# Four pairs of rows of a token group in seven products instead of three, with weight sums made partly by accumulating transfers

## The chip, the cores and the metric

The kernel runs on one core of a Trainium2 chip. The metric is the device time of one execution in microseconds. Work is done by TensorE (PE, with its weight loads PEld), VectorE (DVE), ScalarE (ACT) and GpSimd (POOL); SyncE (SP) issues most transfers, which 16 DMA engines carry out.

## What is computed

The reference is a decoder trunk of two layers for 256 tokens of width 2048. Layer 0 has a retention mixer, layer 1 a short gated convolution; each is followed by a SwiGLU feed-forward network (FFN) with 5632 hidden columns. Every sub-layer has an RMSNorm with a shift and a scale from a conditioning vector, and its output is gated and added to x.

```python
for i in range(DEPTH):
    mod = (c_act @ w_mod[i] + b_mod[i])[:, None, :]
    sh1, sc1, g1, sh2, sc2, g2 = jnp.split(mod, 6, axis=-1)
    h = (rms_norm(x, norm1_g[i]) * (1.0 + sc1) + sh1)
    y = retention_mixer(...) if i % 4 == 0 else short_conv_mixer(...)
    x = x + g1 * y
    h = (rms_norm(x, norm2_g[i]) * (1.0 + sc2) + sh2)
    x = x + g2 * swiglu(h, ffn_w_in[i], ffn_w_out[i])

def swiglu(h, w_in, w_out):
    a, b = jnp.split(h @ w_in, 2, axis=-1)
    return (jax.nn.silu(a) * b) @ w_out
```

The change touches the FFN of layer 1 only. Weights and data are float32.

## The kernel before, in words

**Weights.** All weights lie in `w_all` in the order of use, in chunks of 128 x 2048 (1 MB). `fetch` (L381) has SP load a chunk into one of three `raw` buffers (RAW_BUFS). `prepare` (L387) cuts a chunk into pieces: ACT casts a piece into its high part `hi` (L413), DVE subtracts to get the low part `lo` (L416). `hi` and `lo` have four buffers each (PART_BUFS). A product is three matmuls: data high by weights high, data high by weights low, data low by weights high. `take` (L430) hands pieces to the products and prepares up to two pieces ahead.

**Order.** PE's program is in the order in which the code is written. The instructions of the other engines are put in order by the scheduler when the program is built, and each engine works through its own list; SP issues its transfers in order too.

**The FFN of layer 1** has two parts, over 20 and 24 of the 44 tiles of hidden columns (PART_TILES). The first four tiles of part 0 are done in narrow products together with the norm. Then come groups of the first projection ("token groups"): four in part 0 and six in part 1, each over 512 columns of a and the 512 columns of b that belong to them. A group takes eight pairs of 128-row blocks of the weights (the rows are h's 2048 features), one chunk per pair. Each part ends with its output projections: two groups in part 0, one in part 1 followed by eight narrow products.

**Plain and in sevens.** A pair of row blocks (a, b) by two column blocks (c, d) for two tiles of tokens is eight products of 128 x 128 by 512, `triple` (L1187 to L1189): 24 matmuls. For some pairs (IN_SEVENS in the first projection, OUT_SEVENS in the output) the kernel uses a Strassen-Winograd form with seven products, 21 matmuls, whose inputs are sums of the four data blocks and sums of the four weight blocks. The data sums come from `seven_sums` (L629), once per pair of rows. The weight sums are made anew for each seven by DVE, in `prepare`, into the tile `sums`: L419, L423 and L425. Its four pieces have 512, 1024, 1024 and 1024 columns.

**Banks.** Eight PSUM banks stand in two lanes of four, which groups use in turn. A group's four result banks `x_banks` are in its own lane; the four banks m1, m5, m6, m7 of the sevens (shared by all sevens of a group) are in the other lane, which the group before has to leave.

**Behind a group.** After a group's last seven, ACT and DVE combine the m banks into `y` (L1237 to L1241). `middle` (L1269) then returns three steps that are called when so many tiles of the next group are done: the first half of the results (L1248: the group's banks are added; SiLU L1272, product L1273) after 8, the second half after 8 more, and `turned` after 16 more: PE transposes the results (L1259), ACT and DVE split them into `mids` (L1280, L1281), and where the output uses sevens ACT copies them to `full` (L1284) for `seven_sums`. A plain pair counts 16 tiles, a seven 14.

Of the kernel before, what the change touches and what calls it, by code (L numbers as in the profile page):

```python
# [10 lines left out]
F32 = mybir.dt.float32  # L11
# [3 lines left out]
ALU = mybir.AluOpType  # L15
PSUM = bass.MemoryType.PSUM

P = 128
# [7 lines left out]
DV = 512  # L26
# [38 lines left out]
class Group:  # L65
# [202 lines left out]
def trunk(ctx: ExitStack, tc: tile.TileContext, x_in, c_in, pos_in, w_mod, cols_in, tab_in, w_all, out):  # L268
# [96 lines left out]


    order = [(g, *b) for _, _, g in in_use_order() for b in g.taken()]
    pieces, at_col = [], 0
    for _, _, g in in_use_order():
        width = sum(w for _, _, w in g.blocks())  # L370
        for o in range(-at_col % HALF, width, HALF):
            i = (at_col + o) % CHUNK
            if not g.seven:
                pieces.append(("plain", i))
            elif i == 0:
                pieces += [("seven", n) for n in range(4)]
        at_col += width
    order.reverse()
    ready, used, raws, fetched, n_fetched = [], [0], [], [], [0]

    def fetch():  # L381
        raw = wpool.tile([P, CHUNK], F32, tag="raw", name=name("raw"), bufs=RAW_BUFS)
        nc.sync.dma_start(raw, w_all[n_fetched[0]])
        n_fetched[0] += 1
        fetched.append(raw)

    def prepare(between=None):  # L387
        if prepared[0] == len(pieces):
            return
        kind, i = pieces[prepared[0]]  # L390
        prepared[0] += 1
        if i == 0:
            if not fetched:
                fetch()
            raws[:] = [fetched.pop(0)]
            while first <= units[0] < early and len(fetched) < RAW_BUFS - 1 and n_fetched[0] < w_all.shape[0]:
                fetch()
        full = raws[0]
        if kind == "plain":
            raw = full[:, i : i + HALF]  # L400
        else:
            if i == 0:
                blocks[:] = [spool[0].tile([P, 4, DV], F32, tag="sums", name=name("sums"), bufs=1)]
# [9 lines left out]
        nc.scalar.copy(hi[:, :n], raw)  # L413
        if between:
            between()
        nc.vector.tensor_tensor(lo[:, :n], raw, hi[:, :n].bitcast(F32), op=ALU.subtract)  # L416
        ready.append((hi, lo, n))
        if kind == "seven" and i == 0:
            nc.vector.tensor_tensor(  # L419
                blocks[0][:, 0:2, :].rearrange("p a b -> p (a b)"), full[:, DV : 3 * DV], full[:, : 2 * DV],  # L420
                op=ALU.subtract,
            )
            nc.vector.tensor_tensor(t2, block[2], t1, op=ALU.subtract)  # L423
        elif kind == "seven" and i == 1:
            nc.vector.tensor_tensor(t4, block[3], t2, op=ALU.subtract)  # L425

    blocks, spool = [], []
    prepared = [0]

    def take(group, k, col, width=P):  # L430
# [200 lines left out]
    def seven_sums(full, tag):  # L631

        (a11, a21), (a12, a22) = [[full[:, i, t * P : (t + 1) * P] for t in range(2)] for i in range(2)]
        s = spool[0].tile([P, 4, P], F32, tag="ssum", name=name("ssum"), bufs=1)
        s1, s2, s3, s4 = [s[:, i, :] for i in range(4)]
        nc.vector.tensor_tensor(s1, a21, a22, op=ALU.add)
        nc.vector.tensor_tensor(s2, s1, a11, op=ALU.subtract)
        nc.vector.tensor_tensor(s3, a11, a21, op=ALU.subtract)
        nc.vector.tensor_tensor(s4, a12, s2, op=ALU.subtract)
        dst = spool[0].tile([P, 2, 4, P], F32R, tag=tag, name=name(tag), bufs=1)  # L640
        nc.scalar.copy(dst[:, 0], s)
        nc.vector.tensor_tensor(dst[:, 1], s, dst[:, 0].bitcast(F32), op=ALU.subtract)
        return dst
# [550 lines left out]
    def token_products(steps, act, sums_of, then):  # L1194
# [8 lines left out]
        for n, g in enumerate(steps):  # L1203
            first, last = n == 0, n == len(steps) - 1
            if not g.seven:
# [28 lines left out]
            if g is sevens[-1]:  # L1234
                m1, m5, m6, m7 = [flat(m_banks[i]) for i in ("m1", "m5", "m6", "m7")]
                y11, y12, y21, y22 = values = [value(f"y{i}") for i in range(4)]
                nc.scalar.copy(y11, m1)  # L1237
                nc.vector.tensor_tensor(y12, m6, y11, op=ALU.add)
                nc.vector.tensor_tensor(y21, m7, y12, op=ALU.add)
                nc.vector.tensor_tensor(y12, m5, y12, op=ALU.add)  # L1240
                nc.vector.tensor_tensor(y22, m5, y21, op=ALU.add)  # L1241
# [22 lines left out]
    def middle(values, finals, tag, at, mid, sums_of):  # L1264

        a1, b1, a2, b2 = values

        def product_of(t):
            finals[2 * t]()  # L1269
            finals[2 * t + 1]()  # L1270
            a, b = values[2 * t], values[2 * t + 1]
            nc.scalar.activation(a, a, AF.Silu)  # L1272
            nc.vector.tensor_tensor(b, b, a, op=ALU.mult)  # L1273

        def turned():
            pts = [turned_banks((b1, b2), tag, 2 * i) for i in range(2)]
            for i, pt in enumerate(pts):
                n = at + 2 * i
                t = mid[n // 2]
                nc.scalar.copy(t[:, :, 0, :], pt)  # L1280
                nc.vector.tensor_tensor(t[:, :, 1, :], pt, t[:, :, 0, :].bitcast(F32), op=ALU.subtract)  # L1281
                if n in sums_of:
                    full = fpool.tile([P, 2, S], F32, tag="full", name=name("full"), bufs=1)
                    nc.scalar.copy(full, pt)  # L1284
# [142 lines left out]
```

## Time and profile before

| | |
|---|---|
| runs of the kernel | median 2607.35 us of 3 (2607.01 to 2611.01) |
| the profiled execution, device time | 2605.66 us |
| its span, first to last instruction | 2603.9 us |
| mean granted TensorE clock | 0.998 |
| transfers | 687 MB, mean 264 GB/s |
| matmuls | 14341 |

In the page's forty slices PE shows a nine in all but the first and the last, and DVE goes from sevens and eights to nines in the second half; the DMA engines fall from six to eight tenths to five and six in the last third, which is the FFN of layer 1 (from 1878 us).

How to read it: a row of a group of instructions has line, engine, operation, output and input, shape and count, then busy time, the mean length of one in ns, and the idle time of the engine just before them with what ended it. Lengths of matmuls overlap, so their price is taken from the distance of their starts. In a timeline a row is start, length, engine, line, operation, tiles, shape and how many were merged; in square brackets stands the idle time before it and what ended it. A row of waits has who waited, for whom, total us, times and the longest.

### The profile page before, as it was taken

What the parts mean: (1) busy time and instruction counts of PE and PEld (TensorE: products, weight loads), DVE (VectorE), ACT (ScalarE), POOL (GpSimd) and SP (SyncE); (2) the same over time, 40 slices, a digit from 0 to 9 for tenths busy, and PEclk for the clock granted to TensorE, in tenths of its full rate; (3) what the DMA queues carried; (4) which work ended last, traced back from release to release, by engine and by line L of the source; (5) the groups of instructions that cost most, each with busy time, mean ns of one, the idle gap of its engine ahead of it and who ended that gap; (6) DMA issues with size and microseconds to landing.
All of it is one profiled execution on the core that took longest, in us unless ns stands there. A gap on an engine that the chain in (4) does not pass through costs nothing.

```text
span 2603.9 us, 36702 instructions
## 1 busy us (share of the span) xinstructions
PE 2571.1 (99%) x14341; PEld 2239.5 (86%) x14341; DVE 2178.4 (84%) x2751; ACT 1300.3 (50%) x1757; POOL 129.6 (5%) x230
## 2 busy tenths in 40 slices
PE   7999999999999999999999999999999999999998
PEld 5998889888889888888888898888898888888887
DVE  7998878787698887777777889888889999999984
ACT  5544543444456444334444454444565554555553
POOL 0000000120000010010000100000000000000000
PEclk9999999999999999999999999999999999999999
DMA  9976668777676887888887868877755555555553
GB/s 399 402 278 239 231 229 323 273 284 279 252 286 243 330 324 292 290 307 304 293 296 285 306 236 317 316 296 279 287 179 209 180 208 201 189 202 198 196 195 129
DMA packets 96945, 687.48 MB, mean 264 GB/s; under 512 B 10753, under 2 KB 12545, under 8 KB 13825
## 3 DMA queue, kind: packets, MB, share of 16 engines
q1 hardware_dynamic: 96194, 684.48, 71.2%
q8 instruction: 112, 1.84, 0.3%
q10 hardware_dynamic: 576, 0.66, 0.1%
q14 instruction: 63, 0.52, 0.1%
HBM read 682.99 MB, written 2.10 MB: 263 GB/s over the span
## 4 chain that ended last, share of the span: by engine, by line
PE 66%; issue 28%; DVE 3%; DMA 2%; ACT 1%; POOL 0%; SPq 0%; POOLq 0%; ACTq 0%; DVEq 0%
PE bank L475 29%; PE bank L478 15%; PE bank L514 4%; PE bank L513 4%; PE bank L515 4%; DMA raw<-w_all 2%; PE bank L499 1%; PE bank L498 1%; PE bank L500 1%; PE bank L688 1%; DVE lo L416 1%; PE bank L689 1%; PE bank L543 1%; PE bank L690 1%; PE bank L542 1%
## 5 line engine op out<-in xcount | busy, mean ns | idle before, releaser
L413 ACT CAST hi<-raw 128x1024 fp32r<-128x1024 f32 (+1 forms) x912 | 932.3, 1031 | 904.2 <-DMA raw<-w_all 268.3
L416 DVE TENSOR_TENSOR lo<-raw,hi 128x1024 fp32r<-128x1024 f32 (+1 forms) x912 | 1081.0, 1196 | 281.2 <-ACT hi L413 278.8
L475 PE MATMUL bank<-h,hi 128*128 128x512 f32 x2016 | 699.8, 391 | 0.0
L478 PE MATMUL bank<-h,lo 128*128 128x256 f32 x2016 | 564.4, 280 | 0.0
L475 PEld LDWEIGHTS bank<-h,hi 128*128 128x128 f32 x2016 | 377.0, 187 | 82.5
L327 DVE SCALAR_TENSOR_TENSOR raw<-raw,cb 128x2048 f32<-128x2048 f32 x160 | 365.8, 2286 | 33.0 <-DMA raw<-w_mod 32.6
L478 PEld LDWEIGHTS bank<-h,lo 128*128 128x128 f32 x2016 | 381.0, 189 | 0.0
L475 PE MATMUL bank<-mid,hi 128*128 128x512 f32 x922 | 321.1, 395 | 0.0
L478 PE MATMUL bank<-mid,lo 128*128 128x256 f32 x922 | 256.1, 278 | 0.3 <-DVE lo L416 0.3
L475 PEld LDWEIGHTS bank<-mid,hi 128*128 128x128 f32 x922 | 172.9, 188 | 40.5
L513 PE MATMUL bank<-hi,h 128*128 128x512 f32 x512 | 201.7, 394 | 0.0
L514 PE MATMUL bank<-lo,h 128*128 128x512 f32 x512 | 200.9, 392 | 0.1
L515 PE MATMUL bank<-hi,h 128*128 128x512 f32 x512 | 200.0, 391 | 0.0
L1187 PE MATMUL bank<-hi,h 128*128 128x512 f32 x490 | 191.5, 391 | 0.0
L1189 PE MATMUL bank<-hi,h 128*128 128x512 f32 x490 | 190.7, 389 | 0.0
L1188 PE MATMUL bank<-lo,h 128*128 128x512 f32 x490 | 190.7, 389 | 0.0
L478 PEld LDWEIGHTS bank<-mid,lo 128*128 128x128 f32 x922 | 173.3, 188 | 0.6 <-DVE lo L416 0.6
L475 PE MATMUL bank<-rm,hi 128*128 128x512 f32 x496 | 173.0, 395 | 0.0
L413 ACT CAST hi<-sums 128x1024 fp32r<-128x1024 f32 x84 | 88.4, 1052 | 143.2 <-PE bank L1189 104.0
L416 DVE TENSOR_TENSOR lo<-sums,hi 128x1024 fp32r<-128x1024 f32 x84 | 102.8, 1223 | 50.4 <-ACT hi L413 50.1
L478 PE MATMUL bank<-rm,lo 128*128 128x256 f32 x496 | 137.7, 278 | 0.0
L515 PEld LDWEIGHTS bank<-hi,h 128*128 128x128 f32 x512 | 96.6, 189 | 20.7
(230 smaller groups left out, 4098.1 us busy)
## 6 DMA issues: line engine op xcount, KB each, us to landing
raw<-w_all SPq DMA_DIRECT2D x456, 1024.0 KB, 4.9
raw<-w_mod SPq DMA_DIRECT2D x192, 1024.0 KB, 5.5
x<-x_in SPq DMA_DIRECT2D x4, 512.0 KB, 5.2
decay<-tab_in SPq DMA_DIRECT2D x8, 128.0 KB, 3.4
out<-x SPq DMA_DIRECT2D x4, 256.0 KB, 3.2
out<-x ACTq DMA_DIRECT2D x3, 128.0 KB, 2.6
out<-x SPq DMA_DIRECT2D x1, 384.0 KB, 2.6
out<-x ACTq DMA_DIRECT2D x1, 256.0 KB, 3.2
```

The costliest lines, as they stand in the source:

```text
L327: nc.vector.scalar_tensor_tensor(raw, raw, 1.0, cb, op0=ALU.mult, op1=ALU.mult, accum_out=total)
L413: nc.scalar.copy(hi[:, :n], raw)
L416: nc.vector.tensor_tensor(lo[:, :n], raw, hi[:, :n].bitcast(F32), op=ALU.subtract)
L475: nc.tensor.matmul(pt, hi, h, start=fresh and k == g.ks[0], stop=False, skip_group_check=True)
L478: nc.tensor.matmul(pt[:, 1, :], lo, h[:, 0, :], start=False, stop=last and k == g.ks[-1], skip_group_check=True)
L498: nc.tensor.matmul(pt, hi, h[:, 0, :], start=first, stop=False, skip_group_check=True)
L513: nc.tensor.matmul(flat(pt), a[:, 0, :], hi, start=first, stop=False)
L514: nc.tensor.matmul(flat(pt), a[:, 0, :], lo, start=False, stop=False)
L515: nc.tensor.matmul(flat(pt), a[:, 1, :], hi, start=False, stop=last)
L1187: nc.tensor.matmul(flat(pt), a[:, 0, :], hi, start=first, stop=False, skip_group_check=True)
L1188: nc.tensor.matmul(flat(pt), a[:, 0, :], lo, start=False, stop=False, skip_group_check=True)
L1189: nc.tensor.matmul(flat(pt), a[:, 1, :], hi, start=False, stop=last, skip_group_check=True)
```

## The change

- IN_SEVENS of layer 1 goes from pairs 2, 4, 6 to pairs 2, 3, 5, 6. The output's sevens stay as they are.
- The form of the seven products changes signs, so that all weight sums are additions: B11 + B12, B22 + B12 and so on. The seven's blocks lie in another order in `w_all`, and the seven products come in another order.
- `fetch` issues three more transfers for a chunk that a seven uses: SP loads the first block again into a tile `sums` (128 x 512, two buffers instead of one of 128 x 4 x 512), POOL adds the third block onto the fourth inside `raw`, and POOL adds the fourth block onto `sums`. DVE makes the other two sums by two additions in place in `raw` (L424, L425 of the changed kernel). The pieces have 1024, 1024, 512 and 1024 columns; the last one reads what L424 and L425 have written.
- The first half of a group's results is worked on at once and no longer after 8 tiles, so the turning comes 24 tiles into the next group and not 32.

```diff
-IN_SEVENS = {0: (), 1: (2, 4, 6)}
+IN_SEVENS = {0: (), 1: (2, 3, 5, 6)}
+SUM_BUFS = 2
...
-            return [(a, c, DV), (a, d, DV), (b, d, DV), (b, c, DV)]
+            return [(a, c, DV), (b, c, DV), (b, d, DV), (a, d, DV)]
...
-        nc.sync.dma_start(raw, w_all[n_fetched[0]])
+        src = w_all[n_fetched[0]]
+        nc.sync.dma_start(raw, src)
+        if n_fetched[0] in seven_chunks:
+            sums = spool[0].tile([P, DV], F32, tag="sums", name=name("sums"), bufs=SUM_BUFS)
+            nc.sync.dma_start(sums, src[:, :DV])
+            nc.gpsimd.dma_start(raw[:, 3 * DV :], src[:, 2 * DV : 3 * DV], accum_op=ALU.add)
+            nc.gpsimd.dma_start(sums, src[:, 3 * DV :], accum_op=ALU.add)
+            summed_raw.append(sums)
...
-            block = [full[:, n * DV : (n + 1) * DV] for n in range(4)]
-            t1, t3, t2, t4 = [blocks[0][:, n, :] for n in range(4)]
-            if i < 2:
-                raw = full[:, 2 * DV * i : 2 * DV * i + (DV, 2 * DV)[i]]
-            else:
-                raw = blocks[0][:, 2 * i - 4 : 2 * i - 2, :].rearrange("p a b -> p (a b)")
+                sums_now[:] = [summed_raw.pop(0)]
+            raw = (full[:, : 2 * DV], full[:, 2 * DV :], sums_now[0], full[:, DV : 3 * DV])[i]
...
-        if kind == "seven" and i == 0:
-            nc.vector.tensor_tensor(
-                blocks[0][:, 0:2, :].rearrange("p a b -> p (a b)"), full[:, DV : 3 * DV], full[:, : 2 * DV],
-                op=ALU.subtract,
-            )
-            nc.vector.tensor_tensor(t2, block[2], t1, op=ALU.subtract)
-        elif kind == "seven" and i == 1:
-            nc.vector.tensor_tensor(t4, block[3], t2, op=ALU.subtract)
+        if kind == "seven" and i == 1:
+            b21, b22 = full[:, DV : 2 * DV], full[:, 2 * DV : 3 * DV]
+            nc.vector.tensor_tensor(b22, b22, sums_now[0], op=ALU.add)
+            nc.vector.tensor_tensor(b21, b21, b22, op=ALU.add)
...
-                ("m1", a11), (x_banks[1][0], s4), (x_banks[0][0], a12), ("m5", s1), ("m7", s3), ("m6", s2),
-                (x_banks[0][1], a22),
+                ("m1", a11), (x_banks[0][0], a12), (x_banks[1][0], s4), ("m7", s3), ("m5", s1),
+                (x_banks[0][1], a22), ("m6", s2),
...
-        return [(8, lambda: product_of(0)), (8, lambda: product_of(1)), (16, turned)]
+        product_of(0)
+        return [(8, lambda: product_of(1)), (16, turned)]
```

DVE's list in an inner group, before: the seven at place 2 (from its first sum on), the turned results of the group before, and the plain pair at place 3. A number behind a name is that of the tile.

```order
L419 TENSOR_TENSOR sums_19697<-raw_19695 128x1024
L416 TENSOR_TENSOR lo_19717<-raw_19695,hi_19716 128x1024
L423 TENSOR_TENSOR sums_19697<-raw_19695,sums_19697 128x512
L425 TENSOR_TENSOR sums_19697<-raw_19695,sums_19697 128x512
L416 TENSOR_TENSOR lo_19758<-sums_19697,hi_19757 128x1024
L416 TENSOR_TENSOR lo_19766<-sums_19697,hi_19765 128x1024
L1281 TENSOR_TENSOR mids_18011<-bank_19733,mids_18011 128x2x256
L1281 TENSOR_TENSOR mids_18012<-bank_19738,mids_18012 128x2x256
L416 TENSOR_TENSOR lo_19778<-raw_19775,hi_19777 128x1024
L416 TENSOR_TENSOR lo_19790<-raw_19775,hi_19789 128x1024
```

The same place of the changed kernel, where L416 has become L420: the end of the seven at place 2, from its last sum on (the two L1281 rows, L424 and L636 stand just ahead of it), and the whole seven at place 3.

```order
L425 TENSOR_TENSOR raw_19757<-raw_19757 128x512
L637 TENSOR_TENSOR ssum_19793<-ssum_19793,full_19791 128x128
L638 TENSOR_TENSOR ssum_19793<-full_19791 128x128
L639 TENSOR_TENSOR ssum_19793<-full_19791,ssum_19793 128x128
L420 TENSOR_TENSOR lo_19833<-raw_19757,hi_19832 128x1024
L642 TENSOR_TENSOR msums_3628_19798<-ssum_19793,msums_3628_19798 128x512
L420 TENSOR_TENSOR lo_19850<-raw_19843,hi_19849 128x1024
L420 TENSOR_TENSOR lo_19858<-raw_19843,hi_19857 128x1024
L420 TENSOR_TENSOR lo_19871<-sums_19845,hi_19870 128x512
L424 TENSOR_TENSOR raw_19843<-raw_19843,sums_19845 128x512
L425 TENSOR_TENSOR raw_19843<-raw_19843 128x512
L420 TENSOR_TENSOR lo_19881<-raw_19843,hi_19880 128x1024
```

The sums have moved from the front of a seven to just before its last low part, the turned results and their sums have moved ahead of them, and a second seven follows without a plain pair in between.

POOL's list in the changed kernel over the same group and the next; before, POOL has no instruction here.

```order
L391 DMA sums_19759<-w_all 128x512
L391 DMA sums_19845<-w_all 128x512
L390 DMA raw_19757<-w_all 128x512
L390 DMA raw_19843<-w_all 128x512
L391 DMA sums_19911<-w_all 128x512
L390 DMA raw_19909<-w_all 128x512
```

And SP's list for places 3 to 7 of that group, where one row per chunk stood before:

```order
L386 DMA raw_19843<-w_all 128x2048
L386 DMA raw_19890<-w_all 128x2048
L389 DMA sums_19911<-w_all 128x512
L386 DMA raw_19909<-w_all 128x2048
L389 DMA sums_19971<-w_all 128x512
L386 DMA raw_19969<-w_all 128x2048
L386 DMA raw_20014<-w_all 128x2048
```

The load of `sums` goes ahead of the full load of its own chunk, and each accumulation onto `raw` stands on POOL behind the accumulations onto `sums` that the scheduler has put ahead of it.

More of the change, by code (lines that the diff above doesn't have):

```diff
@@ L367, in trunk @@
     order = [(g, *b) for _, _, g in in_use_order() for b in g.taken()]
-    pieces, at_col = [], 0
+    pieces, at_col, seven_chunks = [], 0, set()
     for _, _, g in in_use_order():
@@ L376, in trunk @@
                 pieces += [("seven", n) for n in range(4)]
+                seven_chunks.add((at_col + o) // CHUNK)
         at_col += width
@@ L402, in prepare @@
             if i == 0:
-                blocks[:] = [spool[0].tile([P, 4, DV], F32, tag="sums", name=name("sums"), bufs=1)]
-            block = [full[:, n * DV : (n + 1) * DV] for n in range(4)]
-            t1, t3, t2, t4 = [blocks[0][:, n, :] for n in range(4)]
-            if i < 2:
-                raw = full[:, 2 * DV * i : 2 * DV * i + (DV, 2 * DV)[i]]
-            else:
-                raw = blocks[0][:, 2 * i - 4 : 2 * i - 2, :].rearrange("p a b -> p (a b)")
+                sums_now[:] = [summed_raw.pop(0)]
+            raw = (full[:, : 2 * DV], full[:, 2 * DV :], sums_now[0], full[:, DV : 3 * DV])[i]
         hi = wpool.tile([P, HALF], F32R, tag="hi", name=name("hi"))
@@ L635, in seven_sums @@
         s1, s2, s3, s4 = [s[:, i, :] for i in range(4)]
-        nc.vector.tensor_tensor(s1, a21, a22, op=ALU.add)
+        nc.vector.tensor_tensor(s1, a21, a22, op=ALU.subtract)
         nc.vector.tensor_tensor(s2, s1, a11, op=ALU.subtract)
         nc.vector.tensor_tensor(s3, a11, a21, op=ALU.subtract)
-        nc.vector.tensor_tensor(s4, a12, s2, op=ALU.subtract)
+        nc.vector.tensor_tensor(s4, a12, s2, op=ALU.add)
         dst = spool[0].tile([P, 2, 4, P], F32R, tag=tag, name=name(tag), bufs=1)
@@ L1239, in token_products @@
                 nc.vector.tensor_tensor(y21, m7, y12, op=ALU.add)
-                nc.vector.tensor_tensor(y12, m5, y12, op=ALU.add)
-                nc.vector.tensor_tensor(y22, m5, y21, op=ALU.add)
+                nc.vector.tensor_tensor(y12, m5, y12, op=ALU.subtract)
+                nc.vector.tensor_tensor(y22, m5, y21, op=ALU.subtract)
         x11, x12, x21, x22 = [flat(x_banks[c][t]) for t in range(2) for c in range(2)]
```

2 lines of the change are left out of this document (1 added, 1 removed).

## The prediction

> **What bounds the kernel now.** I read the engine line of the page first, then windows, then what waits for what. The columns of the windows are the length, then busy us and instructions of PE, PEld, DVE, ACT and POOL, the granted clock, the DMA share and GB/s. The first window is one inner group of the last FFN's first projection, from one turning of results to the next; the second is most of the stage that the change touches.
>
> ```profile
> PE 2571.1 (99%) x14341; PEld 2239.5 (86%) x14341; DVE 2178.4 (84%) x2751; ACT 1300.3 (50%) x1757; POOL 129.6 (5%) x230
> ...
> 2020.93:2063.65 42.72, 42.67 (x193) 35.10 (x191) 39.53 (x48) 24.82 (x29) 0.00 (x0) 1.00 0.56 196
> ...
> 1900.00:2520.00 620.00, 619.62 (x2853) 514.47 (x2853) 561.30 (x683) 355.21 (x424) 0.00 (x0) 1.00 0.55 197
> ```
>
> PE has no idle time in the stage and DVE is busy for 39.5 of a group's 42.7 us, so **PE sets the time and DVE follows closely**. PE's timeline (start, length) gives the price of a matmul:
>
> ```profile
> 2024.31 0.39 PE L1189 MATMUL bank<-hi,rows 128*128 128x512 f32 x1
> 2024.75 0.50 PE L1187 MATMUL bank<-hi,rows 128*128 128x512 f32 x1
> 2025.08 0.39 PE L1188 MATMUL bank<-lo,rows 128*128 128x512 f32 x1
> ...
> 2026.70 0.39 PE L1189 MATMUL bank<-hi,h 128*128 128x512 f32 x1
> 2026.92 0.39 PE L1187 MATMUL bank<-hi,h 128*128 128x512 f32 x1
> ...
> 2032.36 0.39 PE L1187 MATMUL bank<-hi,h 128*128 128x512 f32 x1
> ...
> 2035.99 0.39 PE L1188 MATMUL bank<-lo,rows 128*128 128x512 f32 x1
> ...
> 2037.12 0.39 PE L1187 MATMUL bank<-hi,h 128*128 128x512 f32 x1
> ```
>
> A plain pair of rows is 24 matmuls and runs from 2026.92 to 2032.36 (5.44 us); a seven is 21 and runs to 2037.12 (4.76 us): 0.227 us each. What waits in 1900 to 2520 (us in total, times, longest):
>
> ```profile
> PEld bank L1187 <- ACT full L1284: 3.8, 8, 0.5
> ...
> ACT hi L413 <- PE bank L1189: 210.4, 158, 2.6
> ...
> DVE lo L416 <- ACT hi L413: 55.8, 49, 1.6
> ```
>
> PE itself waits only for a bank of the turned results. ACT waits for PE: there are four buffers for split weight pieces, so the cast of a piece starts when PE has finished the piece four before it. Hence the weights are never further ahead than PE's work on three pieces. This is what I follow through the change. Two rows show the rule and one the margin that it leaves:
>
> ```profile
> 2027.18 1.06 ACT L413 CAST hi<-raw 128x1024 fp32r<-128x1024 f32 x1 [0.76 <-PE bank L1189]
> ...
> 2024.59 2.95 DVE L416 TENSOR_TENSOR lo<-raw,hi 128x1024 fp32r<-128x1024 f32 x3
> 2027.46 1.22 DVE L419 TENSOR_TENSOR sums<-raw 128x1024 f32<-128x1024 f32 x1
> ...
> 2033.69 1.23 DVE L416 TENSOR_TENSOR lo<-sums,hi 128x1024 fp32r<-128x1024 f32 x1 [0.73 <-ACT hi L413]
> ```
>
> The cast at 2027.18 starts 0.09 us after the matmul of 2026.70 has ended. The last piece of a seven has its low part at 2034.92 and PE asks for it at 2035.99: 1.07 us to spare. Behind a seven's four pieces stands, so far, always a plain pair, whose two pieces hold PE for 2.72 us each; a seven's pieces hold it for 1.36 or 0.68 us.
>
> **The change part by part.** The durations (count, busy us, mean ns) are those of the same group:
>
> ```profile
> L416 DVE TENSOR_TENSOR lo<-raw,hi 128x1024 fp32r<-128x1024 f32 x13 | 15.7, 1218 | 0.0
> L413 ACT CAST hi<-raw 128x1024 fp32r<-128x1024 f32 x13 | 13.6, 1052 | 6.1 <-PE bank L1189 5.7 <-DVE lo L416 0.3
> ...
> L425 DVE TENSOR_TENSOR sums<-raw,sums 128x512 f32<-128x512 f32 x3 | 2.1, 687 | 0.0
> ...
> L1281 DVE TENSOR_TENSOR mids<-bank,mids 128x512 fp32r<-128x512 f32 x2 | 1.3, 682 | 0.0
> ...
> L642 DVE TENSOR_TENSOR msums<-ssum,msums 128x512 fp32r<-128x512 f32 x1 | 0.7, 683 | 0.0
> ```
>
> *Matmuls removed.* Ten groups have a fourth seven: 30 matmuls x 0.227 = **-6.8 us**, all on PE's path.
>
> *Results turned 8 tiles sooner.* 8 tiles are 12 matmuls, 2.7 us. The matmul at 2024.75 stands 0.44 us behind its forerunner and the next 0.33: 0.21 + 0.11 = 0.32 us of waiting for the turned bank, eight times. It goes: **-2.6 us**. Behind it the low parts of the weights are the next to be late.
>
> *Sums of weights.* A seven costs DVE 2048 sum elements now (L419, L423, L425) and 1024 then. Queued back to back, the two full and one half low parts at 2024.59 take 2.87 us, so a full one occupies DVE 1.13 us and a half one 0.60. A group's DVE work falls by 1.2 us on each of three sevens and grows by 3 us for the fourth: nearly even. By totals nothing happens. What counts is the order: the last piece of a seven is now the sum that DVE has just made, so add, add, cast, low part follow each other, with DVE idle during the cast, and in places 2-3 and 5-6 one seven stands right behind another.
>
> *The second seven of a pair.* Time 0: PE ends its last matmul on the first piece of the seven ahead. Cast of my first piece 0.08 to 1.13, low part from 1.16. The second piece's cast waits for PE's next six matmuls (1.36 us): 1.44 to 2.50, low part 2.53 to 3.75. Third (half) low part from 3.66, L424 from 4.26, L425 needs its result and runs 4.94 to 5.62. Cast of the last piece 5.65 to 6.70, low part 6.73 to **7.95**. PE has 6+3+6 matmuls of the seven ahead and 6+6+3 of this one: 30 x 0.227 = 6.81, less the 0.16 us by which successive matmuls overlap; the last piece's low part is wanted one matmul later, at **6.87**. PE waits 1.1 us. That is the floor for each pair of sevens, with DVE free of all else.
>
> At places 2-3 DVE isn't free. The turning now falls right before, and between the two sevens stand both L1281 rows (1.28 us), four small sums (0.8) and L642 (0.6). The same walk from the start of the group gives the last piece of the first seven 0.1 us late, the first of the second 0.4, the last of the second 2.0: 2.5 us. With 1.1 at places 5-6 the group waits **3.6 us**. The same walk over the order of before gives margins of 1.07 us for the last piece of a seven and 1.3 for the piece behind it, as the trace has.
>
> *Transfers.* Three quarter-size transfers come to each seven; the two that accumulate are issued by POOL, which no row of before shows. Bounds:
>
> ```profile
> raw<-w_all SPq DMA_DIRECT2D x456, 1024.0 KB, 4.9
> ...
> decay<-tab_in SPq DMA_DIRECT2D x8, 128.0 KB, 3.4
> ...
> out<-x ACTq DMA_DIRECT2D x3, 128.0 KB, 2.6
> ```
>
> At least 2.6 us (half the bytes), at most about 9.8 (two full loads one behind the other); interpolated to 256 KB 3.6, and with half a microsecond for POOL I take 4.1. A seven's raw buffer is now held to its last low part, so the seven at place 5 can load only when that of place 2 is done. In the walk the load is issued at 15.4, has landed at 20.3, its accumulation at 24.4; the cast that needs it would start at about 24.1 to 25. Just covered; every microsecond beyond costs a microsecond per group, two from about 7 on. Since loads now share the 16 engines with more, I put **0.4 us** per group. The new issue work is SP's and POOL's; SP takes 52 more small loads ahead of full ones, whose own buffers come free later, and POOL has nothing else in this stage.
>
> The Trainium skill, page "DMA: Bandwidth & Descriptors", section "Anatomy of one DMA — SWDGE (gpsimd) path", gives a POOL-issued transfer 2.0 us plus its bytes at 436 GB/s. By that 256 KB would take an estimated 2.6 us and the transfer term would be nothing instead of 0.4 us per group; SP's full load would take an estimated 4.4 by it, 4.9 in the row, and no row here shows one of POOL's.
>
> *Other edits.* The fourth pair's row sums (about 1.8 us of DVE) fall in the stage's first 50 us, beside plain projections. In the three output groups sevens stand alone between plain pairs; margin and order there stay near 1 us: nothing.
>
> **Sum.** Per group -0.68 - 0.32 + 3.6 + 0.4 = +3.0 us. Eight groups follow another group: +24. Two (each part's first) have no turning of the same kind before them: -0.7 + 2.2 + 0.4 = +2 each. Together +28 on the profiled execution's 2605.66 us (span 2603.9): 2633.7. The median of the runs is 1.7 us above that execution: **2635 us**.
>
> **Rivals.** *DVE keeps ahead (faster).* If no low part is late, -6.8 - 2.6 = -9.4 us: 2598. For it: the waits above have no row of PE on DVE, and DVE has less to add up per seven. Against: never did two sevens touch, and a last piece has 1.07 us to spare when a plain pair precedes it. The point that decides is 1.0 us of waiting per group: half a microsecond per pair of sevens. About that point lies *no change*: 2602 to 2612.
>
> *Transfers become the wait (much slower).*
>
> ```profile
> q1 hardware_dynamic: 14544, 105.91, 55.1%
> ```
>
> In 1940 to 2480 the engines are busy 55% for 8 MB a group. Four sevens add 3 MB, 37%, so 76% if accumulating is a plain write; with each accumulation counted twice 5 MB, 62%, so 89%. If landing takes 7 us instead of 4.1, the walk gives 48 to 49 us per group: +6 each, 2667; at 10 us +12 each, 2725. The Trainium skill, page "DMA: Bandwidth & Descriptors", section "Issuing engines are not separate DMA queues", says that all queues share the same 16 engines: by it POOL's queue buys no bandwidth, which no row of before can show.
>
> **How the numbers follow.** Forecast 0.63; faster 0.12; about even 0.07; transfers 0.18. Half the waiting I expect gives 2613; the transfer case at 7 us gives 2667. Range 2608 to 2670. About 0.2% (5 us) is what a measurement of this kernel can tell from no change. Slower 0.81, same 0.07, faster 0.12.
>
> **What would show it.** Right: between one turning and the next 45 to 46 us instead of 42.72; PE's longest waits on the low part L420, at the end of the second seven of each pair, 2 us at place 3 and 1.1 at place 6; ACT's casts waiting for DVE's L425; no row of PE waiting for the copy "full". Wrong: groups of 41.7 us with PE idle nowhere (first rival), or casts waiting for the landing of raw or sums and accumulations that land 7 us after their issue (the second).

## The result and the profile after

| kernel | median us | runs | ratio to before [95% interval] |
|---|---|---|---|
| before, beside it | 2607.18 | 4 (2606.63 to 2611.01) | 1 |
| after | 2721.73 | 4 (2718.95 to 2728.16) | 1.0442 [1.0428, 1.0457] |

The change makes the kernel slower by 115 us. The direction was forecast, the size was not: 2635 us, at most 2670.

The page's engine line of after, against PE's 99% and DVE's 84% of before:

```profile
PE 2609.8 (96%) x14311; PEld 2243.4 (83%) x14311; DVE 2170.1 (80%) x2754; ACT 1309.9 (48%) x1780; POOL 222.8 (8%) x334
```

The 30 matmuls are gone (14341 to 14311), yet PE no longer fills the span. Windows of after: one inner group from turning to turning, then the stretch 1900 to 2520 that the prediction showed.

```profile
2031.79:2083.41 51.62, 45.66 (x189) 35.34 (x188) 39.52 (x49) 25.91 (x31) 6.93 (x8) 0.97 0.76 225
1900.00:2520.00 620.00, 555.24 (x2389) 437.34 (x2388) 470.16 (x594) 307.91 (x380) 78.04 (x90) 0.96 0.76 221
```

A group takes 51.6 us instead of 42.72. DVE is busy for as long as before (39.5), so it isn't DVE's work that has grown. The DMA share rose from 0.55 to 0.76. What waits in 1900 to 2520 of after:

```profile
DVE lo L420 <- ACT hi L417: 143.7, 84, 8.1
ACT hi L417 <- DMA raw<-w_all: 139.8, 46, 8.6
...
ACT hi L417 <- DVE raw L425: 82.4, 34, 3.4
...
ACT hi L417 <- PE bank L1189: 67.0, 52, 6.1
...
PEld bank L1188 <- DVE lo L420: 45.7, 51, 1.1
PEld bank L1187 <- ACT hi L417: 43.4, 30, 5.8
```

Read from the bottom: PE waits for low parts and for casts, DVE's low parts wait for the casts, and the casts wait for transfers onto `raw`. Before, ACT's 210 us of waiting were for PE, which was harmless; now 67 are. No row of PE waiting for the copy `full` is left. The transfers of the same stretch, after and then before (KB each, median us from issue to landing):

```profile
q1 hardware_dynamic: 20316, 113.35, 50.8%
q0 software_dynamic: 12816, 23.34, 24.6%
...
raw<-w_all SPq DMA_DIRECT2D x97, 1024.0 KB, 7.0
raw<-w_all POOLq DMA_DIRECT2D x46, 256.0 KB, 5.2
sums<-w_all SPq DMA_DIRECT2D x44, 256.0 KB, 3.5
sums<-w_all POOLq DMA_DIRECT2D x44, 256.0 KB, 7.6
```

```profile
raw<-w_all SPq DMA_DIRECT2D x117, 1024.0 KB, 4.8
```

Loads take 7.0 us instead of 4.8, and an accumulation onto `raw` another 5.2 behind them. The chain behind PE's longest wait, in after's timeline:

```profile
2284.79 0.86 POOL L390 DMA_DIRECT2D raw<-w_all  x1 [5.68 <-DMA raw<-w_all]
...
2294.20 1.04 ACT L417 CAST hi<-raw 128x1024 fp32r<-128x1024 f32 x1 [7.95 <-DMA raw<-w_all]
...
2295.27 1.23 DVE L420 TENSOR_TENSOR lo<-raw,hi 128x1024 fp32r<-128x1024 f32 x1 [7.77 <-ACT hi L417]
...
2295.29 0.79 PE L1187 MATMUL bank<-hi,rows 128*128 128x512 f32 x1 [5.42 <-ACT hi L417]
```

The full load was issued at 2276.8 and took 7.3 us. POOL can issue the accumulation only when it has landed; this one took 9.3 us from issue to landing. The cast starts 0.1 us after the landing, and PE 1.1 us after the cast.

It is the rule and not an exception. A seven's second cast starts 0.1 us after the landing of its accumulation in 28 of the 30 sevens at places 2, 5 and 6 and in 9 of the 12 of the output groups; at place 3 it never does. POOL's list doesn't hold the accumulations up: in all 39 sevens whose load's landing the trace holds, POOL issued the accumulation 0.6 to 0.8 us after it.

### The profile page after: what moved, and what is told of

Read it like the earlier page. It is cut to its first block, busy times and chain, and to the rows that moved or that the text cites. A ratio compares the mean times of both kernels' runs of the same rounds, so it can differ in the third digit from the quotient of the medians.

```text
span 2717.2 us, 37216 instructions
## 1 busy us (share of the span) xinstructions
PE 2609.8 (96%) x14311; PEld 2243.4 (83%) x14311; DVE 2170.1 (80%) x2754; ACT 1309.9 (48%) x1780; POOL 222.8 (8%) x334
## 4 chain that ended last, share of the span: by engine, by line
PE 76%; DMA 10%; DVE 8%; ACT 3%; issue 3%; SPq 0%; POOL 0%; ACTq 0%; POOLq 0%; DVEq 0%
PE bank L475 30%; PE bank L478 15%; DMA raw<-w_all 10%; DVE lo L420 4%; PE bank L513 4%; PE bank L514 4%; PE bank L515 4%; ACT hi L417 3%; PE bank L1188 2%; PE bank L1189 2%; PE bank L1187 2%; PE bank L500 1%; PE bank L499 1%; PE bank L498 1%; PE bank L688 1%
## 5 line engine op out<-in xcount | busy, mean ns | idle before, releaser
L417 ACT CAST hi<-raw 128x1024 fp32r<-128x1024 f32 x964 | 996.5, 1050 | 1137.2 <-DMA raw<-w_all 387.5
L420 DVE TENSOR_TENSOR lo<-raw,hi 128x1024 fp32r<-128x1024 f32 x964 | 1165.5, 1222 | 463.4 <-ACT hi L417 459.1
L513 PE MATMUL bank<-hi,h 128*128 128x512 f32 x512 | 201.7, 394 | 0.0
L514 PE MATMUL bank<-lo,h 128*128 128x512 f32 x512 | 201.0, 393 | 0.0
L515 PE MATMUL bank<-hi,h 128*128 128x512 f32 x512 | 200.1, 391 | 0.0
L1188 PE MATMUL bank<-lo,h 128*128 128x512 f32 x440 | 177.7, 404 | 19.6 <-DVE lo L420 18.9
L1187 PE MATMUL bank<-hi,h 128*128 128x512 f32 x440 | 177.2, 403 | 16.5 <-ACT hi L417 16.4
L1189 PE MATMUL bank<-hi,h 128*128 128x512 f32 x440 | 173.5, 394 | 0.0
L1188 PEld LDWEIGHTS bank<-lo,h 128*128 128x128 f32 x440 | 84.0, 191 | 49.8 <-DVE lo L420 33.7
L1187 PEld LDWEIGHTS bank<-hi,h 128*128 128x128 f32 x440 | 84.1, 191 | 43.1 <-ACT hi L417 26.1
L515 PEld LDWEIGHTS bank<-hi,h 128*128 128x128 f32 x512 | 96.7, 189 | 20.8
```

The lines of the kernel that those rows point to most:

```text
L513: nc.tensor.matmul(flat(pt), a[:, 0, :], hi, start=first, stop=False)
L514: nc.tensor.matmul(flat(pt), a[:, 0, :], lo, start=False, stop=False)
L515: nc.tensor.matmul(flat(pt), a[:, 1, :], hi, start=False, stop=last)
L1187: nc.tensor.matmul(flat(pt), a[:, 0, :], hi, start=first, stop=False, skip_group_check=True)
L1188: nc.tensor.matmul(flat(pt), a[:, 0, :], lo, start=False, stop=False, skip_group_check=True)
L1189: nc.tensor.matmul(flat(pt), a[:, 1, :], hi, start=False, stop=last, skip_group_check=True)
```

## The experiments

Theory T at this point: the loss beyond the forecast is the accumulation onto `raw`, which stands in series between a load and a cast. Rivals: the transfers slow one another and everything else (contention); the order of DVE's work (the prediction's main term) is larger than I took it. All ratios are to the kernel before, run beside them.

| run | sevens at | what differs from after | median us | ratio [interval] |
|---|---|---|---|---|
| e1_no_acc | 2, 3, 5, 6 | no accumulation at all | 2630.84 | 1.0092 [1.0061, 1.0123] |
| e2_apart | 2, 4, 6 | no two sevens side by side | 2681.83 | 1.0287 [1.0257, 1.0317] |
| e3_plain_pool | 2, 3, 5, 6 | POOL's transfers write, don't add | 2676.96 | 1.0269 [1.0239, 1.0298] |
| e4_no_raw_acc | 2, 3, 5, 6 | no accumulation onto `raw` | 2632.25 | 1.0097 [1.0068, 1.0126] |
| e5_split | 2, 3, 5, 6 | a seven's load in two transfers | 2695.43 | 1.0349 [1.033, 1.0369] |
| e6_apart_split | 2, 4, 6 | the same | 2655.57 | 1.0186 [1.0168, 1.0204] |
| e7_apart_no_raw_acc | 2, 4, 6 | no accumulation onto `raw` | 2603.79 | 0.9993 [0.9984, 1.0002] |
| e8_turn24 | 2, 4, 6 | before, with the turning of after | 2603.48 | 0.9992 [0.9984, 1.0001] |
| e9_off_path | 2, 4, 6 | both sums in a tile apart from `raw` | 2603.06 | 0.9986 [0.9978, 0.9995] |
| e10_x_only | 2, 4, 6 | one of them so, the other by DVE | 2620.17 | 1.0054 [1.0041, 1.0067] |
| e11_small_acc | 2, 3, 5, 6 | accumulation onto `raw` of 32 KB | 2659.92 | 1.0206 [1.0188, 1.0224] |
| e12_no_sum_acc | 2, 3, 5, 6 | no accumulation onto `sums` | 2675.75 | 1.0267 [1.0249, 1.0284] |
| e13_pair_2_3 | 2, 3, 5 | as e7 but for the places | 2621.26 | 1.0058 [1.0042, 1.0073] |
| e14_pair_5_6 | 2, 5, 6 | as e7 but for the places | 2620.66 | 1.0055 [1.0041, 1.0069] |
| e15_y_dve | 2, 4, 6 | as e10, DVE's sum earlier | 2627.08 | 1.0075 [1.0062, 1.0089] |

**Transfers or order?** e1 and e4 leave transfers out, e2 undoes the order.

```diff
# e1: both lines go; e4: the first goes
-            nc.gpsimd.dma_start(raw[:, 3 * DV :], src[:, 2 * DV : 3 * DV], accum_op=ALU.add)
-            nc.gpsimd.dma_start(sums, src[:, 3 * DV :], accum_op=ALU.add)
# e2
-IN_SEVENS = {0: (), 1: (2, 3, 5, 6)}
+IN_SEVENS = {0: (), 1: (2, 4, 6)}
# e3: both accumulations
-..., accum_op=ALU.add)
+...)
```

> The changed kernel without its two accumulating transfers per seven (the sums of the weights stay incomplete; the small load by SP, DVE's additions, the order of the pieces and all matmuls stay). Transfer theory (the landing of the accumulations and the loads that they slow make most of the loss; the waits on the order of DVE's work make the +28 us of the prediction): loads land in 4.8 to 5.2 us again, an inner group takes 45 to 46 us instead of 50 to 52, the whole 2630 to 2645 us. Order theory (adjacent sevens and the additions right before the last piece make nearly all of it, the transfers are covered): the group stays at 50 us and the whole above 2700.

> The changed kernel with sevens at places 2, 4, 6 as before; accumulations and the earlier turning stay. Order theory: no seven stands behind another, the waits of PE for a low part go, the group takes 42.3 us or a little more, the whole 2605 to 2615 us. Transfer theory: the accumulations of three sevens still land late and slow the loads; the group takes 44 to 48 us, the whole 2625 to 2665, and ACT still waits for the landing of raw.

> The changed kernel with POOL's two transfers per seven as plain writes of the same bytes (no accumulation, so the sums are not formed). If the cost lies in accumulating (the destination is read and written again): they land in 3.5 to 4.5 us instead of 5.2 and 8.0, loads in about 5.3, the whole 2640 to 2660 us. If it lies in POOL's queue or in the bytes as such: they land as late as before and the whole stays above 2690. Order theory: no change, above 2700.

> The changed kernel without the accumulation onto raw alone (the fourth block stays without the third); the accumulation onto sums stays. Transfer theory: the one onto raw must wait for the full load and stands right before the cast of the second piece, the one onto sums has a buffer to itself and time; most of the transfer loss goes with it: 2640 to 2665 us, loads land in about 6. If the slowed loads (shared engines) matter more than the accumulation in the chain: 2680 or more. Order theory: above 2700.

An inner group of e1, then of e4, and the transfers of e4 and of e2 in 1900 to 2520:

```profile
2030.77:2075.96 45.19, 42.92 (x189) 34.46 (x188) 39.44 (x50) 26.14 (x31) 0.00 (x0) 1.00 0.56 208
```

```profile
2023.95:2069.10 45.15, 42.83 (x189) 34.45 (x188) 39.74 (x50) 26.20 (x31) 3.45 (x4) 1.00 0.74 232
```

```profile
raw<-w_all SPq DMA_DIRECT2D x111, 1024.0 KB, 5.3
...
sums<-w_all POOLq DMA_DIRECT2D x50, 256.0 KB, 6.9
```

```profile
raw<-w_all SPq DMA_DIRECT2D x103, 1024.0 KB, 7.1
raw<-w_all POOLq DMA_DIRECT2D x38, 256.0 KB, 4.7
...
sums<-w_all POOLq DMA_DIRECT2D x37, 256.0 KB, 8.7
```

Without accumulations the kernel is 24 us slower than before, close to the forecast without its transfer term. The accumulation onto `sums` (6.9 us each) changes nothing by itself that the runs can tell, 1.0097 against 1.0092, with the DMA share at 0.74 instead of 0.56. So the remaining 90 us need the accumulation onto `raw`. Setting the sevens apart leaves 1.0287, so order isn't the reason. In e3 writing instead of adding brings back half of the 91 us: both the place in the chain and the adding count. Of the forecasts for T, e1 hit its band; e4 came out below its own (2632, not 2640 to 2665), e2 lay above both of its bands (2682) and e3 between its two (2677).

**Series or contention?** e5 and e6 let the accumulation start before the whole load has landed, e9 and e10 take it off the load's way.

```diff
# e5, e6: the load of a seven's chunk
-        nc.sync.dma_start(raw, src)
+            nc.sync.dma_start(raw[:, 3 * DV :], src[:, 3 * DV :])
+            nc.sync.dma_start(raw[:, : 3 * DV], src[:, : 3 * DV])
# e9 (sums is 128 x 1024 here; B22 is a piece of its own)
+            nc.sync.dma_start(sums[:, :DV], src[:, 3 * DV :])
+            nc.sync.dma_start(sums[:, DV:], src[:, :DV])
+            nc.gpsimd.dma_start(sums[:, :DV], src[:, 2 * DV : 3 * DV], accum_op=ALU.add)
+            nc.gpsimd.dma_start(sums[:, DV:], src[:, 3 * DV :], accum_op=ALU.add)
# e10: the second and the fourth line of e9 go; ahead of L424
+            nc.vector.tensor_tensor(sums_now[0][:, DV:], full[:, :DV], full[:, 3 * DV :], op=ALU.add)
```

> Same result and same bytes as the changed kernel (2,3,5,6), but the 1 MB load of a seven's weights is issued as two: first its last quarter (256 KB, the base of the accumulation), then the other three quarters (768 KB), so that the accumulation onto the last quarter need not wait for the whole load. Theory S (series: the 90 us are the 5.2 us that the accumulation stands between the landing of the whole load and the second cast): the accumulation now runs beside the 768 KB, and the time falls to 2632 to 2650 us, near the 2632 without this accumulation. Theory C (contention: accumulating takes DMA time, 25.6 per cent of the engines, and slows the loads from 4.8 to 7.2 us): bytes and packets are the same, so 2700 to 2720 us stay.

> As e5, with sevens at places 2, 4, 6 as before, so that no two stand side by side. If series and order are the whole of the loss: PE waits neither for the accumulation nor for a second seven; the turning 8 tiles sooner brings -2.6 us and the lighter sums on VectorE up to -0.4 us a group: 2598 to 2606 us, faster than both kernels. Theory C: 2670 to 2690 us, as with the whole load and sevens at 2, 4, 6 (2682).

> Sevens at 2, 4, 6, results turned 24 tiles later, both sums by accumulating transfers as in the change, so as many accumulations and bytes (one 256 KB base load more), but both in a tile of sums of their own whose bases come by loads of their own: no accumulation stands between the landing of the 1 MB load and a cast. The second piece is then B22 alone (512 columns), the third the two sums (1024). Theory S (series: an accumulation onto raw starts only when the load has landed, and the second cast comes a median 4.4 us after the landing when nothing else holds it): 2598 to 2608 us, as without that accumulation (2604). Theory C (contention: accumulating slows the loads for everybody): loads of 7 us and more make the first casts wait, 2630 to 2680 us as in the kernel with sevens at 2, 4, 6 (2682) or with split loads (2656).

> As the one before, but only B12+B22 is formed by an accumulating transfer off the path, and B11+B12 by VectorE (three sums of 512 columns for a seven by VectorE, where the kernel before has 2048 columns in three instructions). Theory S: 2598 to 2606 us; half the accumulations, so theory C gives about half the loss of the one before, if that has any.

e5 and e6 hit neither forecast. By the ratios e5 brings back 24 of the 91 us, and e6 comes to 2656, 26 us under e2. The transfers of e5 suggest why:

```profile
raw<-w_all SPq DMA_DIRECT2D x48, 768.0 KB, 7.0
raw<-w_all SPq DMA_DIRECT2D x48, 256.0 KB, 5.0
raw<-w_all POOLq DMA_DIRECT2D x48, 256.0 KB, 6.2
```

Beside its own other three quarters the first quarter takes 5.0 us, and the accumulation 6.2 more: 11.2 us from issue to the sum, while the other three quarters have landed after 7.0. By these medians the series has become shorter by 1 us only (12.2 in after). e9 decides. Its inner group, its transfers and its waits:

```profile
2018.03:2060.40 42.37, 42.37 (x193) 35.17 (x191) 37.03 (x46) 24.87 (x29) 5.27 (x6) 1.00 0.86 273
```

```profile
raw<-w_all SPq DMA_DIRECT2D x117, 1024.0 KB, 6.7
sums<-w_all SPq DMA_DIRECT2D x80, 256.0 KB, 4.5
sums<-w_all POOLq DMA_DIRECT2D x80, 256.0 KB, 9.2
```

```profile
ACT hi L418 <- PE bank L1190: 204.5, 166, 4.4
...
ACT hi L418 <- DMA raw<-w_all: 27.7, 15, 3.9
```

As many accumulations as in e2 (two to a seven), 9.2 us long by the median (e2: 4.7 and 8.7), loads of 6.7 us (e2: 7.1), the engines 86% busy, and PE waits for nothing: 2603 us against 2682. Contention alone costs nothing here; it costs only where a transfer stands in series. e10 and e15 (below) missed: 2620 and 2627.

**How much of it is length, how much company?**

```diff
# e11
-            nc.gpsimd.dma_start(raw[:, 3 * DV :], src[:, 2 * DV : 3 * DV], accum_op=ALU.add)
+            nc.gpsimd.dma_start(raw[:, 3 * DV : 3 * DV + 64], src[:, 2 * DV : 2 * DV + 64], accum_op=ALU.add)
# e12
-            nc.gpsimd.dma_start(sums, src[:, 3 * DV :], accum_op=ALU.add)
```

> Changed kernel, the accumulation onto raw cut to 64 of its 512 columns (32 KB; the rest of that sum is left out), still behind the whole load. If its time from issue to landing is mostly a fixed part, it still takes 3 us and more and most of the loss stays: 2670 to 2705 us. If it is bytes and packets (an eighth of them), it takes under 2.5 us, within the 4.4 us of slack less the load's, and the time falls to 2632 to 2655 us.

> Changed kernel, only the accumulation onto sums left out (B11+B12 then lacks B12). Theory S: it was free without the other, the accumulation onto raw stays behind the load: 2690 to 2720 us. Theory C (two accumulations of a seven slow each other and the loads): the accumulation onto raw lands in about 4 us and the loads in about 6: 2655 to 2685 us.

Rows of e11, of e12 and of e3, all in 1900 to 2520:

```profile
raw<-w_all SPq DMA_DIRECT2D x106, 1024.0 KB, 5.3
...
raw<-w_all POOLq DMA_DIRECT2D x49, 32.0 KB, 3.5
```

```profile
raw<-w_all SPq DMA_DIRECT2D x102, 1024.0 KB, 6.4
raw<-w_all POOLq DMA_DIRECT2D x48, 256.0 KB, 4.7
```

```profile
raw<-w_all SPq DMA_DIRECT2D x103, 1024.0 KB, 6.3
raw<-w_all POOLq DMA_DIRECT2D x48, 256.0 KB, 4.2
```

An eighth of the bytes takes 3.5 us where after's full accumulation, in the same company, takes 5.2. So much of the length doesn't go by bytes, though how much differs by place (medians of 2.5 against 5.0 at place 2, 5.3 both times at place 6). e11 lay between its two forecasts. e12 lies in the band that I had given to contention: the accumulation onto `sums`, free in e4, costs 46 us when the other one is there (1.0442 less 1.0267), and with it the load (6.4 to 7.0) and the accumulation (4.7 to 5.2) in the chain are longer. One table puts the runs with four sevens in line. The first column is load plus transfer onto `raw`, by the medians shown, over all loads. The second is read from the traces for the sevens alone: the median from the issue of a seven's load (in e5 of its first quarter) to the landing of its transfer, POOL's 0.6 us included.

| load + transfer onto raw, us | of the sevens alone, us | run | ratio |
|---|---|---|---|
| 5.3 + 0 | 6.6 | e4 | 1.0097 |
| 5.3 + 3.5 = 8.8 | 11.1 | e11 | 1.0206 |
| 6.3 + 4.2 = 10.5 | 11.2 | e3 | 1.0269 |
| 6.4 + 4.7 = 11.1 | 10.7 | e12 | 1.0267 |
| 5.0 + 6.2 = 11.2 | 12.4 | e5 | 1.0349 |
| 7.0 + 5.2 = 12.2 | 13.8 | after | 1.0442 |

In the main, the longer the way from the issue of a load to the finished sum, the longer the kernel, whatever lengthens it. One median doesn't give the whole loss: in the first column e12 and e5 are all but equal, and in the second e11 stands out of order. Why loads grow that much in after is not fully settled: a load starts when PE has used up the chunk three before, so late casts also push loads together; the runs don't separate that from the price of the accumulations.

**The other terms.**

```diff
# e7: e4 with
-IN_SEVENS = {0: (), 1: (2, 3, 5, 6)}
+IN_SEVENS = {0: (), 1: (2, 4, 6)}
# e13: (2, 3, 5); e14: (2, 5, 6)
# e8: before, with
-        return [(8, lambda: product_of(0)), (8, lambda: product_of(1)), (16, turned)]
+        product_of(0)
+        return [(8, lambda: product_of(1)), (16, turned)]
```

> Changed kernel with sevens at 2, 4, 6 and without the accumulation onto raw (the sum B12+B22 is left out, the rest is kept). Order theory (the 23 us that remained without any accumulation are the second seven right behind a first): they go, 2598 to 2606 us. Rival: the 23 us come from the new order of blocks and of the seven products, which this kernel keeps: 2620 to 2632 us.

> Kernel before with one part of the change: product 0 of a group's results at once, so that the results turn 24 tiles later, not 32. The step of the prediction: the wait of PE for the copied results at the turning goes, 2.6 us over the kernel: 2604 to 2605.5 us. Rival (the wait only moves to another bank): 2606.5 to 2608 us.

> Changed kernel without the accumulation onto raw (that sum is left out), sevens at 2, 3, 5: three as in the kernel with 2, 4, 6 (2604 us), but two of them side by side. Order theory with the prediction's prices (2.5 us a group at places 2-3, 1.1 at 5-6, ten groups): 2626 to 2632 us. Rival (the loss comes with the number of sevens, four instead of three): 2602 to 2606 us.

> As the one before, with sevens at 2, 5, 6. Order theory with the prediction's prices: 2613 to 2617 us. If a pair costs the same wherever it stands, half of what the four cost over three and the 0.7 us a group that the fourth saves: 2620 to 2623 us. Rival (number): 2602 to 2606 us.

Inner groups of e7, e8, e13 and e14, and PE's waits in 1900 to 2520 of the latter two:

```profile
2020.73:2063.10 42.37, 42.37 (x192) 35.17 (x191) 36.83 (x46) 24.94 (x29) 2.60 (x3) 1.00 0.72 236
```

```profile
2016.91:2059.28 42.37, 42.37 (x193) 35.17 (x191) 39.80 (x49) 24.84 (x29) 0.00 (x0) 1.00 0.54 198
```

```profile
2020.19:2064.16 43.97, 42.94 (x193) 35.10 (x191) 36.87 (x46) 24.81 (x29) 2.61 (x3) 1.00 0.70 227
```

```profile
2026.26:2070.06 43.80, 42.96 (x192) 35.10 (x191) 36.90 (x46) 24.71 (x29) 2.61 (x3) 1.00 0.70 228
```

```profile
PEld bank L1187 <- DVE lo L419: 10.7, 10, 1.1
...
PEld bank L1186 <- ACT hi L416: 6.8, 10, 1.0
```

```profile
PEld bank L1187 <- DVE lo L419: 10.7, 10, 1.1
...
PEld bank L1186 <- ACT hi L416: 5.1, 10, 0.5
```

Three sevens apart have no such wait and a group of 42.37 us (e7 as e8), so the new form of the seven and its order of blocks cost nothing. Between e2 and e7 stands the accumulation onto `raw` alone: 77 us with three sevens apart (1.0287 less 0.9993). The number of sevens isn't what costs either: with three, one pair side by side costs 1.6 us a group at 2-3 and 1.4 at 5-6, in the kernel 17 and 16 us (1.0058 and 1.0055 less 0.9993). The price is nearly the same at both places, not 2.5 and 1.1 as predicted. All of these waits are for the last piece of the pair's second seven: 0.5 to 0.7 us for its cast and 1.1 for its low part, which is the 1.1 of the walk for a pair. e14 hit the band for a price that doesn't depend on the place, e7 the one for order; e13 came out between its two (2621, with 2626 to 2632 for order and 2602 to 2606 for the number of sevens), and e8 half a microsecond below its own.

Last, a version with fewer transfers:

```diff
# e15: sums is 128 x 512 again and made of B12 and B22; m5 comes ahead of m7
+        if kind == "seven" and i == 0:
+            nc.vector.tensor_tensor(full[:, 3 * DV :], full[:, 3 * DV :], full[:, :DV], op=ALU.add)
         nc.vector.tensor_tensor(lo[:, :n], raw, hi[:, :n].bitcast(F32), op=ALU.subtract)
```

> Sevens at 2, 4, 6, results 24 tiles later; B12+B22 by an accumulating transfer into a tile of sums of its own, off the path of the 1 MB load, and B11+B12 by VectorE in the load's own last quarter, before the first piece's low part (in the kernel with 2620 us it stood behind the second piece's, with the third cast waiting for it). Half the transfers of the kernel with 2603 us. If place of VectorE's sum was the cause of 2620: 2598 to 2606 us; if a third sum on VectorE is too much wherever it stands: 2612 to 2622 us.

Waits of e15, then of e10:

```profile
DVE raw L420 <- DMA raw<-w_all: 53.1, 17, 4.2
PEld bank L1189 <- DVE lo L421: 22.0, 16, 2.6
```

```profile
DVE sums L423 <- DMA raw<-w_all: 46.3, 18, 4.5
PEld bank L1188 <- DVE lo L419: 17.5, 16, 2.8
```

Neither forecast held. By these rows the scheduler puts DVE's sum at a place in its list where the load has often not landed; DVE works through its list in order and stands still, and low parts behind it come late. That was not tried apart.

So e9 is the fastest complete version: 0.9986. But e8, three lines on the kernel before, has 0.9992 with an interval that holds it: as far as the runs can tell, what is gained over before is the turning, and the transfers bring nothing.

## Why the prediction was wrong in size

- **Matmuls removed, -6.8 us.** The count is as predicted. It wasn't tried alone, but the sum below closes with it, and so do e4 and e7: four sevens cost 27 us more than three apart (1.0097 less 0.9993), close to 33 less 6.8.
- **Turning sooner, -2.6 us: right.** e8 takes 0.35 us off a group (predicted 0.32) and has 0.9992, about 2 us, with an interval that just reaches 1.
- **Order of DVE's work, 3.6 us a group, 8 x 3.6 + 2 x 2.2 = 33 us in all: right in sum.** e13 and e14 give 17 + 16 = 33, each good to about 5. The split between the places was off (2.5 and 1.1, against 1.6 and 1.4 there and 1.9 and 1.4 in e4), so the close agreement is partly luck. "Half a microsecond per pair" as the point that decides: a pair costs 1.4 to 1.6, so *DVE keeps ahead* falls.
- **Transfers, 0.4 us a group, 4 us in all: this is the step that failed.** They cost 91 us (1.0442 less 1.0092), good to about 9. The other three terms give -2 - 6.8 + 33 = 24 us, which is what e1, without accumulations, measures.

The failing sentence is "Just covered". It was read off one seven, that of place 5, with a load of 4.9 us, half a microsecond for POOL, for which no row stood, and 3.6 us of accumulation. The half microsecond was about right (0.6). Three things were off. First, the lengths: 5.2 us instead of 3.6, and loads of 7.0 instead of 4.9. But the assumed length would not have been covered either: e11's accumulation takes 3.5 us, with POOL's 0.6 just the 4.1 of the prediction, and loses 1.1% over e4.

Second, the places differ. The slack is how long after the landing of its load a seven's second cast starts in e4, which has no accumulation between the two (median over the inner groups whose landing the trace holds). How far PE falls behind at a place is read from the starts of its matmuls: the time from the first one of a place to the first one of the next, less 0.227 us for each (mean of eight groups of after, nine of e4).

| place | 2 | 3 | 4 | 5 | 6 |
|---|---|---|---|---|---|
| slack in e4, us | 2.6 | 9.0 | plain | 3.4 | 4.7 |
| sevens | 5 | 10 | | 5 | 10 |
| PE falls behind in e4, us | 0.1 | 1.9 | 0.0 | 0.0 | 1.4 |
| PE falls behind in after, us | 1.3 | 2.4 | 0.4 | 0.8 | 4.2 |

Place 5 had been put at 3.8 to 4.7; places 2 and 6 hadn't been looked at. POOL's 0.6 and the accumulation's 5.2 exceed the slack at all three, so all three casts come late, but PE doesn't lose as much as a cast is late: casts run ahead of PE. Of the 5.6 us a group that after loses over e4, half falls at place 6, which has the widest slack of the three; its load, though, has grown from 5.1 us to 7.2 (medians at that place), and the seven of place 5 has just been late. What part each of these has was not tried. So "every microsecond beyond costs a microsecond per group" was too simple as well.

Third, the output groups, put at nothing, have the same chain with their twelve sevens. From the first cast of a group's first chunk to that of the next group, the ten groups of the first projection take 64 us longer in after than in e4, and the three output groups 26.

The rival *transfers become the wait* had the mechanism and the sign for it, "casts waiting for the landing of raw". Its mark, accumulations that land after 7 us, was met only by those onto `sums` (7.6), which cost nothing by themselves; those onto `raw` took 5.2. It put loads at their old length and looked at place 5 alone, and gave 2667 us for 7 us and 2725 for 10. That the second is close to the 2722 measured is luck. One of the prediction's sums is off too: half the waiting gives 2615 to 2619 by its own terms, without and with the transfer term, not 2613; neither bound of the range comes from it.

The Trainium skill, page "DMA: Bandwidth & Descriptors", section "Anatomy of one DMA — SWDGE (gpsimd) path", gives a transfer issued by POOL 2.0 us plus its bytes at 436 GB/s, an estimated 2.6 us for 256 KB. The runs show 4.2 to 6.1 for plain writes (the medians of e3) and 4.7 to 9.2 for accumulating ones, so the measurement decides. The same page of the Trainium skill, section "Issuing engines are not separate DMA queues", says that transfers started by any engine run on the same 16 DMA engines and interleave. The runs agree: loads go from 4.8 us (e1) to 5.3 (e4) or 6.4 (e12) with one accumulation to a seven and 6.7 (e9) to 7.1 (e2) with two.

## What to carry to other kernels

A transfer whose source and target are both ready early may take 9 us and cost nothing; one that has to wait for another transfer adds its whole length to that way, and only the slack at the end of it is free, so ask first for what it waits, and give an accumulation a tile and a base of its own. Work out the slack for every place in the loop and for the groups outside it, and not for one place, and set the lengths for a loaded machine: more transfers lengthen the loads that the slack was counted from. Two products with many small pieces should not stand side by side where the next one's preparation can't start before the first one's buffers are free.

## What the runs showed of the hardware

- Accumulating is dear in engine time. In 1900 to 2520 of after, 113.35 MB of loads took 50.8% of the engines and 23.34 MB of accumulations 24.6%: 0.45 and 1.05% for a MB. The accumulations went in 12816 packets; the row of plain writes by POOL in e3 has 7600 for about as many bytes and gives 0.63:

```profile
q0 software_dynamic: 7600, 24.91, 15.8%
```

- Its length goes only in part by its bytes: 3.5 us for 32 KB (e11), 5.2 for 256 KB (after).
- The engines can be 86% busy over a group without any wait on PE (e9).
- Where PE waits, the granted clock falls too: 0.97 in after's group, 1.00 in those of e4 and e9. From 1900 to 2520 it is 0.50 in after for 44 us in all, in e4 never. The first row stands behind PE's longest wait (5.4 us), the second behind two of 0.7 and 0.8 us:

```profile
2292.00:2302.20 10.20, 6.33 (x13) 4.23 (x14) 5.73 (x7) 5.73 (x7) 0.79 (x1) 0.50 0.31 69
2049.60:2053.00 3.40, 3.40 (x10) 2.60 (x9) 2.43 (x3) 1.02 (x2) 0.89 (x1) 0.50 0.87 162
```

- In the first of these stretches most matmuls take 0.63 us, not 0.39. From 1878 us on, the starts behind matmuls longer than 0.45 us are 28 us farther apart in after than 0.227 us each would make, and 3 us in e4. By this estimate about a quarter of the loss that needs the accumulation onto `raw` is the lower clock behind the waits, and the rest the waits; no run tried it apart.
